# Hybrid attention encoder layer: the output projection in two groups of 1024 columns, with six of its sixteen row-pair products formed as seven products of block sums

## The chip, the cores and the metric

The kernel runs on one core of one Trainium2 chip. The metric is the device time of one execution in microseconds (us), the median of several runs. Before the change it is 1386.31 us (three runs, 1385.98 to 1386.63).

## The reference

The reference is one layer of an encoder on 256 tokens of 2048 numbers, in float32. Two attention branches and their gates come from one input projection; they are merged, projected, normed and added to the input, and a squared-ReLU MLP follows:

```
h = rms_norm(x, norm_mix_pre)
proj = h @ w_in                       # q, k, v of both branches, and the gates
oa = differential attention, on = neighbourhood attention
g_a, g_b = split(sigmoid(gates), 2)
mixed = g_a * (oa @ w_branch_a) + g_b * (on @ w_branch_b)
y = mixed @ w_out                     # 256 x 2048 by 2048 x 2048
x = x + rms_norm(y, norm_mix_post)
h = rms_norm(x, norm_mlp_pre)
u = square(relu(h @ w_up))
x = x + rms_norm(u @ w_down, norm_mlp_post)
```

The change touches `y = mixed @ w_out`, and what comes just before and behind it.

## The kernel before

The 256 tokens are two halves t0 and t1 of 128. Every float32 operand of a product is split in a high part of the matmul's own type and the remainder, the low part, and a product is three matmuls into one PSUM bank: high x high, high x low, low x high. ScalarE makes the high part (a copy that rounds), VectorE the low part (a subtraction). Weights come on SyncE's DMA queue in pieces of 1 MB, into pools of three buffers each for the raw piece, the high part and the low part (`wp`).

There are three ways of grouping a projection. `wgroup` (input projection, MLP up) has the weights stationary. `agroup` has the activations stationary and 512 columns of weights moving, in four pieces of four blocks of 128 rows each; both token halves accumulate in a bank of their own. `wide_group` (gates and branches) works on 1024 columns and on row pairs, that is 256 rows at a time, which makes a 2 x 2 block product of tokens (t0, t1) x rows by rows x columns. In the plain form (`eight`) a row pair is eight products. In the other (`seven`) it is seven products of sums of blocks, whose results five operations combine at the end (`combine`: a ScalarE copy and four VectorE operations over banks 0, 4, 5 and 6; the plain products go to banks 1, 2, 3 and 7, whose results are added piece by piece). `pair_weights` loads a pair's weights and, for `seven`, forms the sums of weight blocks on VectorE and splits them too; the two sums' parts are in a pool of five tiles (`mid`). `sums_of` forms the sums of activation blocks. The second to fourth gate groups use `seven` for three of their eight pairs (`MIXED`).

Around the output projection the order is as follows. The branch groups of the second column half (`bb1` last) end with the merged values in pages (a pool of 27 pages of 4 KB per partition). `mixed_T` transposes them on TensorE and splits them (`mh`, `ml`), the first half's earlier, the second half's 16 transposes at the start of y. The temporary pool `tmp` is opened again, `gpost` and `x2` (the post-norm gain and the residual input) are loaded on SP's queue. Then y runs as four `agroup`s of 512 columns (matmuls L230 to L232). Each group's `y_evac` squares the bank on ScalarE with a running sum, multiplies it by the gain on VectorE (L902), and in the last group calls `post_norm(t)`: a reduction, two small steps, and a power on GpSimd (L89).

In the last group t0 is finished before t1 begins. `residual_parts(t, c)` takes 512 columns: the residual on VectorE (L853), four transposes on TensorE (L860), and the split of each with the next norm's gain on ScalarE (L869) and VectorE (L870), into `hT2`, which the MLP's up projection reads. `between` puts the first two such blocks of t0 into t1's products, before the sixth and the seventh of the eight that are left; `tc.issue_after` ties the products behind them to that place. For t1 the first block (`residual_parts(1, 0)`) stands alone between y's last matmul and the first matmul of the up projection (L192); the other blocks are interleaved with the first up group.

A planner orders the instructions of each engine by a simulated timeline, with program order as priority, and gives pool tiles their places; each engine then runs its queue in that order.

Of the kernel before, what the change touches and what calls it, by code (L numbers as in the profile page):

```python
# [11 lines left out]
F32 = mybir.dt.float32  # L12
F32R = mybir.dt.float32r
AF = mybir.ActivationFunctionType
ALU = mybir.AluOpType
AX = mybir.AxisListType

P = 128
D = 2048
T = 256  # L20
KD = D // P
# [17 lines left out]
def encoder_layer(ctx: ExitStack, tc: tile.TileContext, a, out):  # L39
    nc = tc.nc  # L40
# [7 lines left out]
    temps = ctx.enter_context(ExitStack())  # L48
    tmp = temps.enter_context(tc.tile_pool(name="tmp", bufs=6))
    mm = ctx.enter_context(tc.tile_pool(name="mm", bufs=NMM, space=PSUM))  # L50
    ms = ctx.enter_context(tc.tile_pool(name="ms", bufs=8 - NMM, space=PSUM))

    def page(shape, dt, name):
        return pages.tile(shape, dt, tag="pg", name=name)
# [4 lines left out]
    def t2k(name, dt=F32):  # L59
        return tmp.tile([P, 2, T], dt, tag="t2k", name=name, bufs=7)  # L60
# [9 lines left out]
    def junk512(n):  # L70
        return tmp.tile([P, 2, T], F32, tag="t2k", name=n, bufs=7)
# [596 lines left out]
            nc.vector.tensor_sub(c12, self.ps[4], c12)  # L668
            nc.vector.tensor_sub(c22, self.ps[4], c21)

    def wide_group(name, kinds, view, stat7, stat8, mm_banks, z, piece, each=None):


        any7 = any(s for _, s in kinds)
        pr = Products(name, mm_banks, range(8) if any7 else (1, 2, 3, 7))
        for n, (i, seven) in enumerate(kinds):
            if each:
                each(n)
            w = pair_weights(view(i), f"{name}_{i}", seven)
            if seven:  # L680
                final = not any(s for _, s in kinds[n + 1 :])
                pr.seven(partial(stat7, i), w, final)
                if final:
                    pr.combine(z)
                continue
            end = n == len(kinds) - 1
            for which in range(4):
                pr.eight(partial(stat8, i), w, which, end)
                if end:
                    b, t, half = PLAIN[which]  # L690
                    piece(t, half, pr.ps[b], any7)

    def sums_of(p1, p2, name, hi=None, lo=None):

        a11, a21, a12, a22 = p1[:, :P], p1[:, P:], p2[:, :P], p2[:, P:]
        s = t2k(f"{name}s").rearrange("p a (b c) -> p (a b) c", b=2)
        nc.vector.tensor_sub(s[:, 0], a21, a22)
        nc.vector.tensor_sub(s[:, 1], a11, a21)
        nc.vector.tensor_sub(s[:, 2], s[:, 0], a11)
        nc.vector.tensor_add(s[:, 3], a12, s[:, 2])  # L700
        parts_ = page([P, 2, 4, P], F32R, name)
        nc.scalar.copy(parts_[:, 0], s)
        nc.vector.tensor_sub(parts_[:, 1], s, parts_[:, 0].bitcast(F32))
        return parts_
# [24 lines left out]
    ALL8 = [(i, 0) for i in range(8)]  # L729
    mT = []  # L730
    mixed = []

    def mixed_T(h, n):

        mh, ml = page([P, 4, T], F32R, f"mh{h}{n}"), page([P, 4, T], F32R, f"ml{h}{n}")
        for b in range(2):
            pt = bank(f"mT{h}{n}{b}")
            for j in range(2):
                for t in range(2):
                    c = (n * 4 + b * 2 + j) * P  # L740
                    nc.tensor.transpose(
                        pt[:, j * T + t * P : j * T + (t + 1) * P],
                        mixed[h][t].rearrange("p a b -> p (a b)")[:, c : c + P],
                        ident,
                    )
            at = slice(b * 2, b * 2 + 2)
            src = pt.rearrange("p (j q) -> p j q", j=2)
            nc.scalar.copy(mh[:, at], src)
            nc.vector.tensor_sub(ml[:, at], src, mh[:, at].bitcast(F32))
        mT.append((mh, ml))  # L750

    for h in range(2):
# [59 lines left out]
        mixed.append(gate[0])  # L812
    for n in range(2):
        mixed_T(1, n)
    stage.close()
    temps = ctx.enter_context(ExitStack())
    tmp = temps.enter_context(tc.tile_pool(name="tmp", bufs=6, reuse_waits="tile"))


    def mstat(k, t):  # L820
        mh, ml = mT[k // 4]
        return mh[:, k % 4, t * P : (t + 1) * P], ml[:, k % 4, t * P : (t + 1) * P]

    gpost = [page([P, 1024], F32, f"gpost{h}") for h in range(2)]
    for h in range(2):
# [4 lines left out]
    for t in range(2):  # L830
        for h in range(2):
            nc.sync.dma_start(
                x2[t * 2 + h], x[t * P : (t + 1) * P, h * 1024 : (h + 1) * 1024]
            )
    yw = [page([P, 1024], F32, f"yw{i}") for i in range(4)]
    ssy = [small(4, f"ssy{t}") for t in range(2)]

    ss2 = [small(4, f"ss2{t}") for t in range(2)]
# [10 lines left out]
    def residual_parts(t, c, after=None):  # L849
        cs = slice((c % 2) * 512, (c % 2 + 1) * 512)  # L850
        xt = x2[t * 2 + c // 2][:, cs]
        with tc.issue_after(after) if after else nullcontext():
            nc.vector.scalar_tensor_tensor(  # L853
                xt, yw[t * 2 + c // 2][:, cs], ry[:, t : t + 1], xt, op0=ALU.mult, op1=ALU.add
            )
        for h in range(2):
            pt = bank(f"h2T_t{t}{c}{h}")
            for i in range(2):
                kk = h * 2 + i
                last = nc.tensor.transpose(  # L860
                    pt[:, i * P : (i + 1) * P], xt[:, kk * P : (kk + 1) * P], ident
                )
            for i in range(2):
                k = c * 4 + h * 2 + i
                d = hT2[k // 2][:, k % 2]
                src = pt[:, i * P : (i + 1) * P]
                hi = d[:, t * P : (t + 1) * P]
                g = g_mlp[:, k : k + 1]
                act = nc.scalar.activation(hi, src, AF.Copy, scale=g)  # L869
                vec = nc.vector.scalar_tensor_tensor(  # L870
                    d[:, T + t * P : T + (t + 1) * P],
                    src,
                    g,
                    hi.bitcast(F32),
                    op0=ALU.mult,
                    op1=ALU.subtract,
                )
        return last.ins, act.ins, vec.ins

    def between(i):  # L880
        return residual_parts(0, i - 5)[0] if i in (5, 6) else None

    def mlp_squares(t):
        for c in range(4):
            cs = slice((c % 2) * 512, (c % 2 + 1) * 512)
            j = junk512("jx").rearrange("p a b -> p (a b)")
            nc.scalar.activation(
                j, x2[t * 2 + c // 2][:, cs], AF.Square, accum_out=ss2[t][:, c : c + 1]
            )
# [3 lines left out]
        nc.vector.tensor_reduce(s2, ss2[t], axis=AX.X, op=ALU.add)  # L893
        inv_rms(s2, D, f"r2{t}", r2[:, t : t + 1])

    for cg in range(4):

        def y_evac(t, ps, cg=cg):
            j = junk512("jy").rearrange("p a b -> p (a b)")
            nc.scalar.activation(j, ps, AF.Square, accum_out=ssy[t][:, cg : cg + 1])  # L900
            cs = slice((cg % 2) * 512, (cg % 2 + 1) * 512)
            nc.vector.tensor_mul(yw[t * 2 + cg // 2][:, cs], ps, gpost[cg // 2][:, cs])  # L902
            if cg == 3:
                post_norm(t)

        agroup(
            a["w_out"], cg * 512, mstat, KD, y_evac, f"y{cg}", *((2, between) if cg == 3 else ())
        )
    mlp_squares(0)
    tail = [residual_parts(1, 0)]  # L910
    after = {1: tail[0][1:]}
# [72 lines left out]
    for k in range(2, NK - LAST):  # L984
        w = dweight(k)
# [83 lines left out]
```

## Time and profile before

| | before |
|---|---|
| median of three runs | 1386.31 us |
| the profiled execution | 1386.53 us |
| its span, first to last instruction | 1384.7 us |
| mean granted TensorE clock | 0.996 |
| matmuls, weight loads | 6861 each |
| output projection, first to last matmul | 570.2 to 660.2 us |
| first matmul of the up projection | 665.0 us |

A row of the timeline gives the start in us from the span's start, the duration in us, the engine, the line of the kernel, the operation, what is written from what, and how many instructions were merged into the row; in brackets stands how long the engine had been idle and who released it. Matmul records overlap, since matmuls are pipelined: a 512-column one is shown as 0.39 us long, and they start about 0.23 us apart. A row of a table by stretch gives the stretch, its length, busy us with instruction counts for PE (matmuls), PEld (weight loads), DVE (VectorE), ACT (ScalarE) and POOL (GpSimd), the granted clock, the DMA share and GB/s.

### The profile page before, as it was taken

What the parts mean: (1) busy time and instruction counts of PE and PEld (TensorE: products, weight loads), DVE (VectorE), ACT (ScalarE), POOL (GpSimd) and SP (SyncE); (2) the same over time, 40 slices, a digit from 0 to 9 for tenths busy, and PEclk for the clock granted to TensorE, in tenths of its full rate; (3) what the DMA queues carried; (4) which work ended last, traced back from release to release, by engine and by line L of the source; (5) the groups of instructions that cost most, each with busy time, mean ns of one, the idle gap of its engine ahead of it and who ended that gap; (6) DMA issues with size and microseconds to landing.
All of it is one profiled execution on the core that took longest, in us unless ns stands there. A gap on an engine that the chain in (4) does not pass through costs nothing.

```text
span 1384.7 us, 16956 instructions
## 1 busy us (share of the span) xinstructions
PE 1363.7 (98%) x6861; PEld 1157.6 (84%) x6861; DVE 851.7 (62%) x1093; ACT 659.6 (48%) x923; POOL 7.9 (1%) x19
## 2 busy tenths in 40 slices
PE   7999999999999999999899999999999999999997
PEld 6888888888888888888788888888888888888886
DVE  6878866677857876654755554555566554444445
ACT  7455455544643544443754444444465443333332
POOL 0000000000000000000000000000000000000000
PEclk9999999999999999999999999999999999999999
DMA  8675745564655565766456565556555556555551
GB/s 292 204 230 165 205 153 182 178 180 156 206 187 184 208 223 172 248 225 195 127 178 212 161 205 184 196 189 192 182 183 208 186 191 235 183 196 199 186 200 71
DMA packets 105198, 265.11 MB, mean 191 GB/s; under 512 B 15008, under 2 KB 16288, under 8 KB 96928
## 3 DMA queue, kind: packets, MB, share of 16 engines
q1 hardware_dynamic: 104976, 264.03, 58.2%
q8 instruction: 53, 0.87, 0.3%
q14 instruction: 25, 0.20, 0.0%
q10 hardware_dynamic: 144, 0.01, 0.0%
HBM read 261.92 MB, written 3.92 MB: 192 GB/s over the span
## 4 chain that ended last, share of the span: by engine, by line
PE 98%; DVE 1%; DMA 0%; ACT 0%; SPq 0%; issue 0%; DVEq 0%; POOLq 0%; POOL 0%; ACTq 0%
PE u_p L192 17%; PE u_p L193 9%; PE acc L975 8%; PE acc L974 8%; PE acc L973 8%; PE qa_p L192 2%; PE ka_p L192 2%; PE qn_p L192 2%; PE kn_p L192 2%; PE ga L639 2%; PE y_p L232 2%; PE y_p L231 2%; PE ga L642 2%; PE ga L641 2%; PE y_p L230 2%; PE gb L642 2%
## 5 line engine op out<-in xcount | busy, mean ns | idle before, releaser
L192 PE MATMUL u_p<-h2T,u_h 128*128 128x512 f32 x1024 | 359.3, 397 | 1.0 <-DVE h2T L870 1.0
L193 PE MATMUL u_p<-h2T,u_l 128*128 128x256 f32 x1024 | 284.1, 280 | 0.0
L117 DVE TENSOR_TENSOR d_l<-d_w,d_h 128x1024 fp32r<-128x1024 f32 x128 | 151.1, 1222 | 164.1 <-ACT d_h L116 163.7
L117 DVE TENSOR_TENSOR u_l<-u_w,u_h 128x1024 fp32r<-128x1024 f32 x128 | 151.1, 1222 | 145.1 <-ACT u_h L116 143.8
L192 PEld LDWEIGHTS u_p<-h2T,u_h 128*128 128x128 f32 x1024 | 191.7, 188 | 45.7 <-DVE h2T L870 1.2
L116 ACT CAST d_h<-d_w 128x1024 fp32r<-128x1024 f32 x128 | 127.9, 1047 | 191.5 <-PE acc L975 187.9
L974 PE MATMUL acc<-d_l,uh 128*128 128x512 f32 x512 | 199.0, 389 | 0.0
L975 PE MATMUL acc<-d_h,ul 128*128 128x512 f32 x512 | 198.9, 389 | 0.0
L973 PE MATMUL acc<-d_h,uh 128*128 128x512 f32 x512 | 198.2, 389 | 0.0
L193 PEld LDWEIGHTS u_p<-h2T,u_l 128*128 128x128 f32 x1024 | 193.5, 189 | 1.3
L116 ACT CAST u_h<-u_w 128x1024 fp32r<-128x1024 f32 x128 | 128.0, 1048 | 123.1 <-PE u_p L192 62.3
L974 PEld LDWEIGHTS acc<-d_l,uh 128*128 128x128 f32 x512 | 96.1, 188 | 20.1
L973 PEld LDWEIGHTS acc<-d_h,uh 128*128 128x128 f32 x512 | 96.1, 188 | 19.9
L975 PEld LDWEIGHTS acc<-d_h,ul 128*128 128x128 f32 x512 | 96.1, 188 | 19.8
L117 DVE TENSOR_TENSOR y_l<-y_w,y_h 128x1024 fp32r<-128x1024 f32 x32 | 37.9, 1222 | 30.9 <-ACT y_h L116 30.9
L116 ACT CAST y_h<-y_w 128x1024 fp32r<-128x1024 f32 x32 | 32.0, 1047 | 40.9 <-PE y_p L232 32.6
L230 PE MATMUL y_p<-y_h,mh 128*128 128x512 f32 x128 | 50.1, 391 | 0.0
L231 PE MATMUL y_p<-y_l,mh 128*128 128x512 f32 x128 | 49.9, 390 | 0.0
L232 PE MATMUL y_p<-y_h,ml 128*128 128x512 f32 x128 | 49.8, 390 | 0.0
L192 PE MATMUL qa_p<-hT,qa_h 128*128 128x512 f32 x128 | 47.7, 419 | 1.2 <-DVE hT L275 1.2
L192 PE MATMUL qn_p<-hT,qn_h 128*128 128x512 f32 x128 | 45.9, 400 | 0.0
L192 PE MATMUL kn_p<-hT,kn_h 128*128 128x512 f32 x128 | 45.4, 398 | 0.0
(549 smaller groups left out, 2378.3 us busy)
## 6 DMA issues: line engine op xcount, KB each, us to landing
u_w<-in_w_up SPq DMA_DIRECT2D x64, 1024.0 KB, 5.4
d_w<-in_w_down SPq DMA_DIRECT2D x64, 1024.0 KB, 5.0
y_w<-in_w_out SPq DMA_DIRECT2D x16, 1024.0 KB, 5.3
ka_w<-in_w_in SPq DMA_DIRECT2D x8, 1024.0 KB, 6.7
va_w<-in_w_in SPq DMA_DIRECT2D x8, 1024.0 KB, 5.2
qn_w<-in_w_in SPq DMA_DIRECT2D x8, 1024.0 KB, 5.1
kn_w<-in_w_in SPq DMA_DIRECT2D x8, 1024.0 KB, 5.1
vn_w<-in_w_in SPq DMA_DIRECT2D x8, 1024.0 KB, 5.1
```

The source lines that it names most:

```text
L116: nc.scalar.copy(hi[part], raw[part])
L117: nc.vector.tensor_sub(lo[part], raw[part], hi[part].bitcast(F32))
L192: nc.tensor.matmul(ps[b], hi[:, k % 4, cs], mv, start=(k == 0), stop=False)
L193: nc.tensor.matmul(ps[b][:, :T], lo[:, k % 4, cs], mv[:, :T], start=False, stop=(k == nk - 1))
L230: nc.tensor.matmul(ps[t], sh, hi[:, k % 4], start=(k == 0), stop=False)
L231: nc.tensor.matmul(ps[t], sh, lo[:, k % 4], start=False, stop=False)
L232: nc.tensor.matmul(ps[t], sl, hi[:, k % 4], start=False, stop=(k == nk - 1))
L639: nc.tensor.matmul(self.ps[i], sh, wh[:, blk], start=i not in self.begun, stop=False)
L642: nc.tensor.matmul(self.ps[i], sl, wh[:, blk], start=False, stop=last)
L973: nc.tensor.matmul(acc[t][c], uh[:, k % 4, ts_], hi[:, 0, cs], start=(k == 0), stop=False)
L974: nc.tensor.matmul(acc[t][c], uh[:, k % 4, ts_], lo[:, 0, cs], start=False, stop=False)
L975: nc.tensor.matmul(acc[t][c], ul[:, k % 4, ts_], hi[:, 0, cs], start=False, stop=(k == NK - 1))
```

## The change

The output projection becomes two `wide_group`s of 1024 columns. Row pairs 1, 3 and 5 of each go as `seven`, the other five as `eight`. The activation sums for these pairs (`msum`) are formed in `mixed_T`, from a copy of the transposed values in a page. The results of the sevens are combined into `yw`; each piece of the plain products is then added to it by `y_piece`, squared from there and multiplied in place by the gain. The piece's scratch and the sums get pages, and `tmp` is opened again after y instead of before it.

In the second group the last two pairs are kept back and run together, one quarter (token half and column half) after the other, t0's two first; `between` is called within t1's quarters, and residual blocks of t0 stand before the sixth and seventh of t1's eight products, as before.

```diff
-    def wide_group(name, kinds, view, stat7, stat8, mm_banks, z, piece, each=None):
+    def wide_group(name, kinds, view, stat7, stat8, mm_banks, z, piece, each=None, between=None):
...
             end = n == len(kinds) - 1
+            if between and n == len(kinds) - 2:
+                ahead = (i, w)
+                continue
+            last = None
             for which in range(4):
-                pr.eight(partial(stat8, i), w, which, end)
+                if between and end:
+                    b, t, half = PLAIN[which]
+                    for m, (ii, ww) in enumerate((ahead, (i, w))):
+                        for k in range(2):
+                            if t:
+                                last = between((which - 2) * 4 + m * 2 + k) or last
+                            with tc.issue_after(last) if last else nullcontext():
+                                pr.add(b, stat8(ii, k, t), ww, k * 2 + half, m + k == 2)
+                else:
+                    pr.eight(partial(stat8, i), w, which, end)
                 if end:
                     b, t, half = PLAIN[which]
                     piece(t, half, pr.ps[b], any7)
...
-        s = t2k(f"{name}s").rearrange("p a (b c) -> p (a b) c", b=2)
+        s = page([P, 4, P], F32, f"{name}s")
...
+            i = h * 4 + n * 2 + b
+            if i in (1, 3, 5):
+                f = page([P, 512], F32, f"mf{i}")
+                nc.scalar.copy(f, pt)
+                msum[i] = sums_of(f[:, :T], f[:, T:], f"ms{i}")
...
-    for cg in range(4):
-
-        def y_evac(t, ps, cg=cg):
-            j = junk512("jy").rearrange("p a b -> p (a b)")
-            nc.scalar.activation(j, ps, AF.Square, accum_out=ssy[t][:, cg : cg + 1])
-            cs = slice((cg % 2) * 512, (cg % 2 + 1) * 512)
-            nc.vector.tensor_mul(yw[t * 2 + cg // 2][:, cs], ps, gpost[cg // 2][:, cs])
-            if cg == 3:
+    for g in range(2):
+
+        def y_piece(t, half, ps, summed, g=g):
+            z = yw[t * 2 + g][:, half]
+            nc.vector.tensor_add(z, z, ps)
+            j = page([P, 512], F32, f"jy{g}{t}{half}")
+            c = g * 2 + half
+            nc.scalar.activation(j, z, AF.Square, accum_out=ssy[t][:, c : c + 1])
+            nc.vector.tensor_mul(z, z, gpost[g][:, half * 512 : (half + 1) * 512])
+            if g and not half:
                 post_norm(t)
 
-        agroup(
-            a["w_out"], cg * 512, mstat, KD, y_evac, f"y{cg}", *((2, between) if cg == 3 else ())
-        )
+        wide_group(
+            f"y{g}",
+            [(0, 0), (1, 1), (2, 0), (3, 1), (4, 0), (5, 1), (6, 0), (7, 0)],
...
+            mstat7,
+            mstat8,
+            (1, 2, 3, 7),
+            [yw[g], yw[2 + g]],
+            y_piece,
+            between=between if g else None,
+        )
+    stage.close()
+    temps = ctx.enter_context(ExitStack())
+    tmp = temps.enter_context(tc.tile_pool(name="tmp", bufs=6, reuse_waits="tile"))
```

More of the change, by code (lines that the diff above doesn't have):

```diff
@@ L731, in encoder_layer @@
     mixed = []
+    msum = {}
     def mixed_T(h, n):
@@ L814, in encoder_layer, with mstat8, mstat7 @@
         mixed_T(1, n)
[L815 to L822, printed above, removed]
+    def mstat8(i, k, t):
+        mh, ml = mT[i // 2]
+        k = i % 2 * 2 + k
+        return mh[:, k, t * P : (t + 1) * P], ml[:, k, t * P : (t + 1) * P]
+    def mstat7(i, n):
+        if n < 3:
+            return mstat8(i, int(n > 0), n // 2)
+        return msum[i][:, 0, n - 3], msum[i][:, 1, n - 3]
     gpost = [page([P, 1024], F32, f"gpost{h}") for h in range(2)]
@@ L834, in encoder_layer @@
             )
-    yw = [page([P, 1024], F32, f"yw{i}") for i in range(4)]
+    yw = [page([P, 2, 512], F32, f"yw{i}") for i in range(4)]
     ssy = [small(4, f"ssy{t}") for t in range(2)]
@@ L853, in residual_parts @@
             nc.vector.scalar_tensor_tensor(
-                xt, yw[t * 2 + c // 2][:, cs], ry[:, t : t + 1], xt, op0=ALU.mult, op1=ALU.add
+                xt, yw[t * 2 + c // 2][:, c % 2], ry[:, t : t + 1], xt, op0=ALU.mult, op1=ALU.add
             )
@@ L894, in mlp_scale @@
         inv_rms(s2, D, f"r2{t}", r2[:, t : t + 1])
-    for cg in range(4):
-        def y_evac(t, ps, cg=cg):
-            j = junk512("jy").rearrange("p a b -> p (a b)")
-            nc.scalar.activation(j, ps, AF.Square, accum_out=ssy[t][:, cg : cg + 1])
-            cs = slice((cg % 2) * 512, (cg % 2 + 1) * 512)
-            nc.vector.tensor_mul(yw[t * 2 + cg // 2][:, cs], ps, gpost[cg // 2][:, cs])
-            if cg == 3:
-                post_norm(t)
-        agroup(
-            a["w_out"], cg * 512, mstat, KD, y_evac, f"y{cg}", *((2, between) if cg == 3 else ())
-        )
+    for g in range(2):
[7 more added lines that the diff above has]
+            if g and not half:
+                post_norm(t)
+        wide_group(
+            f"y{g}",
+            [(0, 0), (1, 1), (2, 0), (3, 1), (4, 0), (5, 1), (6, 0), (7, 0)],
+            lambda i, c=g * 1024: a["w_out"][i * T : (i + 1) * T, c : c + 1024].rearrange(
+                "(k p) c -> p k c", p=P
+            ),
+            mstat7,
[4 more added lines that the diff above has]
+            between=between if g else None,
+        )
+    stage.close()
+    temps = ctx.enter_context(ExitStack())
+    tmp = temps.enter_context(tc.tile_pool(name="tmp", bufs=6, reuse_waits="tile"))
     mlp_squares(0)
```

## The prediction

> **What bounds the kernel now.** I read the page's busy times and its chain of waits first, then a table by stretch of time around the output projection, and then the timeline of the projection's end.
>
> ```profile
> PE 1363.7 (98%) x6861; PEld 1157.6 (84%) x6861; DVE 851.7 (62%) x1093; ACT 659.6 (48%) x923; POOL 7.9 (1%) x19
> ...
> PE 98%; DVE 1%; DMA 0%; ACT 0%; SPq 0%; issue 0%; DVEq 0%; POOLq 0%; POOL 0%; ACTq 0%
> ```
>
> The first row is busy time by engine, the second the share of each in the chain that ended last: TensorE is the kernel. A change pays if it takes TensorE instructions away, and costs wherever it makes TensorE wait. The table by stretch shows the last two gate groups of the kernel before and then the whole output projection, y. Its columns are the stretch, its length, and busy us with instruction counts for PE, PEld, DVE, ACT, POOL.
>
> ```profile
> 441.60:483.00 41.40, 41.40 (x185) 34.28 (x184) 35.97 (x34) 21.81 (x17) 0.00 (x0) 1.00 0.60 206
> 483.00:524.50 41.50, 41.50 (x185) 34.38 (x184) 32.43 (x29) 20.54 (x17) 0.00 (x0) 1.00 0.62 203
> 570.00:660.20 90.20, 90.16 (x410) 74.36 (x408) 49.46 (x58) 38.87 (x56) 0.55 (x1) 1.00 0.66 222
> ```
>
> The gate groups already run as the change wants y to run: five row pairs in the plain form (8 products of 3 matmuls, 24) and three as seven products (21), so 5 x 24 + 3 x 21 = 183 matmuls; the count of 185 takes in instructions cut by the edges. TensorE was busy in all of the 41.40 us, so one 512-column matmul costs 41.40 / 183 = 0.2262 us, a plain pair 5.43 and a pair of seven 4.75. In y TensorE is busy without a gap for 90.16 us. What waits stands behind it:
>
> ```profile
> 653.81 0.60 ACT L900 ACTIVATE jy<-y_p 128x512 f32<-128x512 f32 x1 [3.44 <-PE y_p L232]
> 654.30 0.19 ACT L900 ACTIVATION_READ_ACCUMULATOR jy<-y_p 128x1 f32 x1
> 654.53 0.69 DVE L902 TENSOR_TENSOR yw<-y_p,gpost 128x512 f32<-128x512 f32 x1 [2.72 <-ACT jy L900]
> ...
> 656.13 1.42 DVE L853 SCALAR_TENSOR_TENSOR x<-yw,ry,x 128x512 f32<-128x512 f32 x2 [0.66 <-POOL ry L89]
> ...
> 657.01 0.60 PE L860 MATMUL h2T_t<-ident,x 128*128 128x128 f32 x4
> ...
> 660.20 0.60 ACT L900 ACTIVATE jy<-y_p 128x512 f32<-128x512 f32 x1
> 660.29 0.35 DVE L870 SCALAR_TENSOR_TENSOR h2T<-h2T_t,g_mlp,h2T 128x128 fp32r<-128x128 f32 x1 [0.17 <-ACT h2T L869]
> ...
> 660.92 0.69 DVE L902 TENSOR_TENSOR yw<-y_p,gpost 128x512 f32<-128x512 f32 x1 [0.28 <-ACT jy L900]
> ...
> 663.34 0.66 PE L860 MATMUL h2T_t<-ident,x 128*128 128x128 f32 x4 [3.17 <-DVE x L853]
> 664.99 0.80 PE L192 MATMUL u_p<-h2T,u_h 128*128 128x512 f32 x1 [0.99 <-DVE h2T L870]
> ```
>
> Each row is start, duration, engine and line. Token half t0 ends at 653.8; its norm and residual run beside t1's products and are ready at 656.13 + 0.74 = 656.87 (half of the 1.42 of two, with their overlap), 0.14 before its transposes start at 657.01. For t1 nothing covers the same steps: TensorE waits 3.17 and 0.99 us.
>
> **The change part by part.**
>
> *Matmuls removed.* Three of eight pairs in each of two groups go from 24 to 21: 6 x 3 = 18 matmuls x 0.2262 = **-4.07 us**, on the path because y has no gap. Weight loads go with their matmuls. The 16 transposes of the merge and the 8 of t0's residual stay; so do the bytes loaded.
>
> *Sums of weights and activations.* They go to VectorE and ScalarE and cost nothing where TensorE stays ahead. What one pair of seven costs, from the gate group:
>
> ```profile
> 452.28 1.76 DVE L617 TENSOR_TENSOR ga_3l<-ga_3r,ga_3h 128x1536 fp32r<-128x1536 f32 x1 [1.44 <-ACT ga_3h L613]
> 453.95 1.22 DVE L614 TENSOR_TENSOR ga_6t<-ga_6r 128x1024 f32<-128x1024 f32 x1
> 455.09 2.28 DVE L610 TENSOR_TENSOR ga_4l<-ga_4r,ga_4h 128x2048 fp32r<-128x2048 f32 x1
> 457.29 1.22 DVE L623 TENSOR_TENSOR ga_3el<-ga_3t,ga_3eh 128x1024 fp32r<-128x1024 f32 x1
> 458.42 0.68 DVE L615 TENSOR_TENSOR ga_6t<-ga_6t,ga_6r 128x512 f32<-128x512 f32 x1
> ...
> 459.81 0.39 PE L641 MATMUL ga<-ga_3el,hs 128*128 128x512 f32 x1
> ```
>
> VectorE needs 1.22 + 2 x 0.68 + 1.76 + 2 x 1.22 = 6.8 us for a pair of seven and 2.28 for a plain one. A group has 3 x 6.8 + 5 x 2.28 = 31.8, and its four combining and eight piece operations, about 0.69 each, bring 8.3: 40 by durations, which the gate group holds in 35.97 busy us (neighbours overlap) of 41.40. So VectorE goes from 49.46 / 90.2 to nearly nine tenths, and the cover is thin: ga_3el ends at 458.51 and is first used at 459.81, a lead of 1.30. Group y0 carries more than that gate group did:
>
> ```profile
> L749 DVE TENSOR_TENSOR ml<-mT,mh 128x512 fp32r<-128x512 f32 x4 | 2.5, 682 | 0.0
> ...
> L703 DVE TENSOR_TENSOR hs<-hs0s,hs 128x512 fp32r<-128x512 f32 x1 | 0.7, 685 | 0.0
> L697 DVE TENSOR_TENSOR hs3s<-hf 128x128 f32<-128x128 f32 x1 | 0.3, 293 | 0.0
> ```
>
> The last transposes of the merge are split in 2.5, and the sums of pair 5's activations take 4 x 0.29 + 0.69 = 1.8 (those of pairs 1 and 3 come a stage earlier). That is 4.3 more against a lead of 1.30, an idle 1.44 before ga_3l, and 1.22 + 2.28 of work for later pairs that was placed ahead of ga_3el. Bounds: 0 if later work gives way, 4.3 - 1.3 - 1.4 = 1.6 if it doesn't. I take **+0.2**, nearer to 0, since both gate groups lost nothing. Less than 0 is excluded: TensorE has no gap there to win back.
>
> *The moved pool and pages.* Temporaries reopen after y instead of before it; the square's scratch and the sums take pages. No row shows these; the nearest are the 35.97 and 32.43 rows, where the same two weight pools were open, and TensorE waited for nothing. I take 0; a page that comes late would hold x's or gpost's load on SP's queue, with y's weights behind it.
>
> *The end of t0.* A piece was: square from PSUM (0.60 + 0.19), then multiply (0.69). It becomes: add the partial result (nearest row L902, 0.69, the same size and engine), then square, then multiply in place, which must wait for the square. So t0's residual is 0.69 later against a slack of 0.14: TensorE, whose next product is ordered behind these transposes, waits 0.55. VectorE is fuller then than it was: pair 5's four combining operations (2.7), the first up weights (two pieces of 1.22) and the other half's add and multiply all fall in the 5 us before. If one weight piece is ahead of the add, the wait is 0.55 + 1.22 = 1.8. I take **+0.9**, bounds 0.5 and 1.8. What is late next is the t1 tail: the whole shift passes on to it.
>
> *The end of t1.* The add comes before the square on a bare chain: +0.69. In the kernel before, the square could start at 660.20 although VectorE was busy with t0's evacuations until 660.64; the add is on VectorE and must wait for these, which themselves start later while t1's first half brings an add and a multiply among them (2 x 0.69). Bounds 0.69 and 0.69 + 0.44 + 0.69 = 1.8; I take **+1.1**. ScalarE's squares of the residual go into the same idle time as before.
>
> *The clock.* The same table, in steps of 1 us, with the granted clock as the third number from the end:
>
> ```profile
> 664.00:665.00 1.00, 0.01 (x1) 0.01 (x1) 1.00 (x4) 0.47 (x3) 0.00 (x0) 0.97 0.00 0
> 665.00:666.00 1.00, 1.00 (x3) 0.91 (x4) 0.88 (x5) 1.00 (x3) 0.54 (x1) 0.50 0.00 0
> 666.00:667.00 1.00, 1.00 (x4) 0.81 (x4) 1.00 (x3) 1.00 (x2) 0.00 (x0) 0.50 0.00 0
> 667.00:668.00 1.00, 1.00 (x6) 0.90 (x5) 1.00 (x2) 0.48 (x1) 0.00 (x0) 0.50 0.00 0
> 668.00:669.00 1.00, 1.00 (x7) 0.96 (x6) 1.00 (x1) 0.62 (x2) 0.00 (x0) 0.82 0.07 16
> ```
>
> After the idle stretch TensorE runs at half clock for 0.03 x 2 + 3 + 0.18 x 2 = 3.4 us, nearly all of it with matmuls queued: 1.7 us lost. The loss can become less than this if part of the 3.4 us falls into a longer wait, so the bounds are -1.7 and 0. I take 0, the same loss again, since three runs within 0.65 us speak for one that comes back each time. [...]
>
> *The sum.* -4.07 + 0.2 + 0.9 + 1.1 = **-1.87 us** against the profiled execution, 1386.53. That execution is 0.22 above the median of the runs, 1386.31; from the median it is 1384.44. **Forecast: 1384.4 us**, 0.14% less. A measurement of this kernel can tell about 0.2%, 2.77 us, from no change, so this counts as no change.
>
> **The rivals.**
>
> *The slow stretch is hidden.* The wait for t1 grows from 3.2 us by about 1 and ends at another moment; if the clock has dropped well before TensorE resumes, some or all of the 1.7 us is spent waiting. 1384.4 - 1.7 = 1382.7. For it: the drop came only at about 664.97, at the very first up matmul, so that any shift can only shorten what is lost. Against it: the stretch may be tied to the idle time itself.
>
> *The tail costs only its two adds.* 0.5 for t0, 0.7 for t1, nothing at the start: -4.07 + 1.2 = -2.87, 1383.4. For it: the planner orders each engine's work and the add needs only one free slot. Against it: t0's evacuations filled VectorE until 0.44 after t1's last matmul already.
>
> *VectorE becomes the bound.* Place: the low parts of the summed weights (the second and third pair of seven in y0, the first and second in y1). If the 4.3 us of additional work aren't absorbed, each is late by the 1.6 above and VectorE never gets ahead again: 4 x 1.6 = 6.4 in place of 0.2 gives 1384.4 + 6.2 = 1390.6, slower. It decides from a lateness of about 1.2 at each of the four (4.64 in all: 1.87 won and 2.77 over). For it: the 1.30 lead. Against it: 36 of 41.4 us without one wait, and the first rows of that table start behind similar work.
>
> *All of it is given back.* t0 waits 1.8, t1 loses 1.8, the start 0.5: 1386.3, no change.
>
> **How the numbers follow.** The forecast case has 0.57, the hidden slow stretch 0.16, the adds alone 0.13, all given back 0.07, VectorE as bound 0.07. The forecast case's own range goes from its low bounds (-4.07 + 1.2, 1383.4) to its high ones (-4.07 + 1.6 + 1.8 + 1.8 = +1.1, 1387.4). The range for all is 1382.4 to 1387.4: it takes in the hidden stretch with 0.3 to spare, and leaves out the slower case and the corners. Faster by over 0.2% (below 1383.5): 0.16 + 0.13 and 0.04 of the forecast case, 0.33. Slower by over 0.2% (above 1389.1): the VectorE case, 0.07. Within it: 0.60.
>
> **What would show it.** Right: y's matmuls 366 instead of 384, the two groups at about 0.2262 each with no wait in y0; a wait of TensorE of 0.5 to 1.8 us before t0's first transposes; a wait of 4 to 5 us before t1's. Wrong: waits of y's matmuls for L623 or L617; no wait before t0's transposes; a shorter half-clock stretch behind the tail; loads of x or gpost that hold SP's queue so long that y's matmuls wait for a split.

## The result, and the profile after

The changed kernel takes 1395.59 us (median of four runs, 1394.78 to 1395.78) against 1386.14 for the kernel before (four runs, 1384.69 to 1386.63): ratio 1.0067, 95% interval 1.0055 to 1.0079. It is 9.45 us slower, where 1.87 less was forecast. Its profiled execution is the median run, 1395.59, with a span of 1393.8.

The page of the changed kernel, busy times and the chain of waits:

```profile
PE 1364.9 (98%) x6843; PEld 1157.1 (83%) x6843; DVE 888.7 (64%) x1138; ACT 672.5 (48%) x927; POOL 7.9 (1%) x19
...
PE 96%; DVE 2%; ACT 1%; issue 0%; DMA 0%; SPq 0%; POOL 0%; DVEq 0%; POOLq 0%; ACTq 0%
```

The 18 matmuls are gone (6861 to 6843), and yet TensorE is busy 1.2 us longer: some of its matmuls ran slower. Its share of the chain fell from 98 to 96%. What it waited for between 300 and 720 us (before, only the first and the last of these kinds were there, 3.2 and 1.0):

```profile
PE h2T_t L884 <- DVE x L877: 8.0, 2, 4.2
PE y L639 <- ACT y_4h L609: 2.1, 1, 2.1
PE y L641 <- DVE y_4l L610: 1.4, 1, 1.4
PE u_p L192 <- DVE h2T L894: 0.4, 1, 0.4
```

From y's first matmul to the first of the up projection it is 104.40 us (569.59 to 673.99) instead of 94.82 (570.17 to 664.99), 9.58 more: all of the loss lies here. It has two places. The first, in the first group (timeline; SPq is the DMA queue):

```profile
579.23 1.76 DVE L617 TENSOR_TENSOR y_3l<-y_3r,y_3h 128x1536 fp32r<-128x1536 f32 x1 [4.60 <-ACT y_3h L613]
...
587.32 2.29 DVE L610 TENSOR_TENSOR y_4l<-y_4r,y_4h 128x2048 fp32r<-128x2048 f32 x1 [0.88 <-ACT y_4h L609]
587.34 0.96 PE L639 MATMUL y<-y_4h,mh 128*128 128x512 f32 x3 [2.14 <-ACT y_4h L609]
589.53 1.22 DVE L614 TENSOR_TENSOR y_1t<-y_1r 128x1024 f32<-128x1024 f32 x1
589.64 0.38 SPq L606 DMA_DIRECT2D y_5r<-in_w_out  x1
589.67 0.79 PE L641 MATMUL y<-y_4l,mh 128*128 128x512 f32 x1 [1.36 <-DVE y_4l L610]
590.26 0.63 PE L642 MATMUL y<-y_4h,ml 128*128 128x512 f32 x1
590.69 0.63 PE L639 MATMUL y<-y_4h,mh 128*128 128x512 f32 x1
```

TensorE waits 2.14 and 1.36 us for pair 4, and then runs matmuls 0.43 apart instead of 0.23 until 595.4 (granted clock 0.50 from 590 to 595, 1.00 from 596 on). The row that tells why is y_1t: the first sums of pair 1's weights, whose piece was cast at 564, are formed only at 589.53, though VectorE stood idle for 4.60 us before 579.23. Without them TensorE had no other products left, and pairs 1 and 3 held two of the three raw buffers, so that pair 5's load left only at 589.64, when pair 4's piece was done with. The loads of gpost and x (574.47 to 577.74 on SPq) were not in the way: pair 4's load left ahead of them, at 574.05, and took 5.1 us to land.

The second place is the end of y:

```profile
657.49 0.69 DVE L924 TENSOR_TENSOR yw<-yw,y 128x512 f32<-128x512 f32 x1
658.62 0.69 DVE L924 TENSOR_TENSOR yw<-yw,y 128x512 f32<-128x512 f32 x1 [0.44 <-PE y L642]
659.23 0.69 DVE L928 TENSOR_TENSOR yw<-yw,gpost 128x512 f32<-128x512 f32 x1
659.83 0.68 DVE L924 TENSOR_TENSOR yw<-yw,y 128x512 f32<-128x512 f32 x1
660.43 0.68 DVE L928 TENSOR_TENSOR yw<-yw,gpost 128x512 f32<-128x512 f32 x1
661.30 0.69 DVE L928 TENSOR_TENSOR yw<-yw,gpost 128x512 f32<-128x512 f32 x1
662.72 1.41 DVE L877 SCALAR_TENSOR_TENSOR x<-yw,ry,x 128x512 f32<-128x512 f32 x2 [0.66 <-POOL ry L89]
663.52 1.02 PE L884 MATMUL h2T_t<-ident,x 128*128 128x128 f32 x4 [3.81 <-DVE x L877]
...
672.45 1.11 PE L884 MATMUL h2T_t<-ident,x 128*128 128x128 f32 x4 [4.16 <-DVE x L877]
673.99 0.80 PE L192 MATMUL u_p<-h2T,u_h 128*128 128x512 f32 x1 [0.42 <-DVE h2T L894]
```

t0's last product is added at 658.62 and t0's transposes run at 663.52: TensorE waits 3.81 us. Between them VectorE's queue holds the addition and the multiply of t1's first piece (659.83, 661.30), and TensorE had only five matmuls of t1 behind t0's last product, not the 15 that the kernel before has: in the order that the planner wrote, ten others stand ahead of it. Then t1's wait, 4.16. With both waits the granted clock falls from 1.00 to 0.50; with the second (table by stretch in steps of 1 us, granted clock third from the end):

```profile
670.00:671.00 1.00, 0.00 (x0) 0.00 (x0) 0.93 (x4) 0.00 (x1) 0.00 (x0) 0.75 0.00 0
...
676.00:677.00 1.00, 1.00 (x6) 0.90 (x5) 1.00 (x2) 0.64 (x1) 0.00 (x0) 0.50 0.00 0
677.00:678.00 1.00, 1.00 (x7) 0.95 (x6) 1.00 (x1) 0.62 (x2) 0.00 (x0) 0.84 0.00 0
```

This stretch goes from about 670.5 to 677.3, 6.8 us, twice the 3.4 of the kernel before; there is one of 6.8 in the first group (588.6 to 595.4) and one of 3.4 behind t0's wait (663.7 to 667.1), where the kernel before has none (1.00 from 570.0 to 660.2).

### The profile page after: what moved, and what is told of

It is laid out like the page before. It is cut to its first block, busy times and chain, and to the rows that moved or that the text cites. A ratio compares the mean times of both kernels' runs of the same rounds, so it can differ in the third digit from the quotient of the medians.

```text
span 1393.8 us, 16981 instructions
## 1 busy us (share of the span) xinstructions
PE 1364.9 (98%) x6843; PEld 1157.1 (83%) x6843; DVE 888.7 (64%) x1138; ACT 672.5 (48%) x927; POOL 7.9 (1%) x19
## 4 chain that ended last, share of the span: by engine, by line
PE 96%; DVE 2%; ACT 1%; issue 0%; DMA 0%; SPq 0%; POOL 0%; DVEq 0%; POOLq 0%; ACTq 0%
PE u_p L192 17%; PE u_p L193 9%; PE acc L1014 8%; PE acc L1013 8%; PE acc L1012 8%; PE qa_p L192 2%; PE ka_p L192 2%; PE qn_p L192 2%; PE kn_p L192 2%; PE ga L641 2%; PE ga L642 2%; PE ga L639 2%; PE gb L642 2%; PE gb L641 2%; PE gb L639 2%; PE y L641 2%
## 5 line engine op out<-in xcount | busy, mean ns | idle before, releaser
L192 PE MATMUL ka_p<-hT,ka_h 128*128 128x512 f32 x128 | 45.0, 398 | 0.0
L997 ACT ACTIVATE u<-up_s 128x256 f32<-128x256 f32 x64 | 25.1, 418 | 25.3 <-DVE up_s L996 25.2
L255 ACT COPY up_r<-u_p 128x256 f32<-128x256 f32 x64 | 23.6, 369 | 26.1 <-PE u_p L193 26.0
L193 PE MATMUL qn_p<-hT,qn_l 128*128 128x256 f32 x128 | 35.9, 281 | 0.0
L193 PE MATMUL kn_p<-hT,kn_l 128*128 128x256 f32 x128 | 35.7, 280 | 0.0
```

The lines of the kernel that those rows point to most:

```text
L192: nc.tensor.matmul(ps[b], hi[:, k % 4, cs], mv, start=(k == 0), stop=False)
L193: nc.tensor.matmul(ps[b][:, :T], lo[:, k % 4, cs], mv[:, :T], start=False, stop=(k == nk - 1))
L255: nc.scalar.copy(r, ps[:, T:])
L997: nc.scalar.activation(u[:, b], s, AF.Square)
```

## The experiments

My theory was that what makes the first place is the order in which the page pool hands out its pages: in the order of the program, so that a tile called for later in the program gets none before those called for earlier. Pair 1's sums, called for with the first group's weights, would then stand behind the pages of the merge's last transposes and of gpost and x. For the second place I had three suspects: the queue orders around t0's norm, the combination just ahead of it, and VectorE's load. The rival throughout was the load: VectorE has too much to do, whatever the order.

All runs are timed against the kernel before on the same chip; the difference is in us of medians. The runs were made on several chips, so rows are best compared by this column.

| run | what it is | median | differs by | ratio, 95% |
|---|---|---|---|---|
| after | the change | 1395.59 | +9.45 | 1.0055 to 1.0079 |
| e1 | first group's weights asked for earlier | 1389.75 | +3.33 | 1.0016 to 1.0037 |
| e2 | square's scratch in the bank | 1399.56 | +13.14 | 1.0084 to 1.0112 |
| e3 | e1 and e2 | 1392.58 | +6.16 | 1.0033 to 1.0061 |
| e4 | t1's products behind t0's | 1394.86 | +8.44 | 1.0050 to 1.0075 |
| e5 | e1, t0's norm ahead of t1's piece | 1388.27 | +2.07 | 1.0005 to 1.0023 |
| e6 | e5 and e4's order | 1387.66 | +1.46 | 1.0001 to 1.0019 |
| e7 | e6, multiply not in place, u's parts later | 1389.01 | +2.81 | 1.0009 to 1.0027 |
| e8 | e1, second group plain | 1385.54 | -0.66 | 0.9984 to 1.0002 |
| e9 | e8, MLP squares behind t1's | 1384.03 | -2.36 | 0.9976 to 0.9994 |
| e10 | the change, second group plain | 1391.73 | +5.34 | 1.0025 to 1.0050 |
| e11 | e6, sevens earlier, squares as e9 | 1391.18 | +4.79 | 1.0025 to 1.0050 |
| e12 | e11, residual first | 1391.51 | +5.12 | 1.0024 to 1.0051 |
| e13 | e8, MLP squares' scratch in pages | 1384.60 | -1.43 | 0.9980 to 0.9998 |
| e14 | e6, squares as e9 | 1387.60 | +1.57 | 1.0000 to 1.0018 |
| e15 | e14 with five sevens | 1386.16 | +0.13 | 0.9992 to 1.0009 |

**e1, the order of the pages.**

```diff
+    made = {i: pair_weights(a["w_out"][i * T : (i + 1) * T, :1024]..., f"y0_{i}", bool(i % 2)) for i in range(4)}
     for n in range(2):
         mixed_T(1, n)
```

> The weights of the first group's first four row pairs are asked for, in program order, ahead of the merge's last transposes; nothing else is changed. Theory (pages): the pool hands its pages out in program order, so the sums of pair 1's weights stood behind the parts of the merge's last transposes and the loads of gpost and x. If so, the two waits in the first group (2.14 and 1.36 us) and the half-clock stretch behind them (2.8 us lost) go: 1395.6 - 6.3 = 1389.3 us, and perhaps 1 to 2 less as VectorE carries less arrears into the second group. Rival (load): VectorE simply has more work in the first group than TensorE's time; then the hole only moves to another operand and the time stays at 1394 to 1396 us.

Measured 1389.75, 5.84 us less than the change. The order of calls is all that differs, and the sums come 33 us earlier (VectorE's timeline), on an engine that has the same work:

```profile
556.01 1.22 DVE L614 TENSOR_TENSOR y_1t<-y_1r 128x1024 f32<-128x1024 f32 x1 [5.14 <-DMA y_1r<-in_w_out]
```

The waits of TensorE in e1; of the first group's 3.5 us nothing is left, 0.4 us at 628.7 us, in the second group, is new, and t0's 3.81 and t1's 3.93 stay (7.7 in two):

```profile
PE h2T_t L890 <- DVE x L883: 7.7, 2, 3.9
PE u_p L192 <- DVE h2T L900: 0.4, 1, 0.4
PE y L641 <- DVE y_4l L610: 0.4, 1, 0.4
```

The load is ruled out for the first place. e10, below, shows the same loss alone. That it is the pool that holds the sums is not shown apart: program order is also the planner's priority, and e1 moves both. For the pool speaks that VectorE idled with the piece at hand, which priority alone does not explain, and that in e13, below, a change of pool alone moves other tiles.

**e2 and e3, the scratch pages of the second group.**

```diff
-            j = page([P, 512], F32, f"jy{g}{t}{half}")
-            nc.scalar.activation(j, z, AF.Square, accum_out=...)
+            nc.scalar.activation(ps, z, AF.Square, accum_out=...)
```

> The square's scratch output goes back into the PSUM bank that was just read instead of a page; nothing else is changed. Theory (pages): in the second group the sums of pair 1's weights stood behind the first group's four scratch pages. Without them these sums come some 10 us earlier, pair 7's low part no longer comes late, and the 3.81 us wait before t0's first transposes falls to 0.6 to 1.8 us: 1392.4 to 1393.6 us, with the hole in the first group unchanged. Rival (load): VectorE is full from 587 us on whatever the order, and the time stays within 0.5 us of 1395.6.

> Both edits: the first four row pairs' weights are asked for ahead of the merge's last transposes, and the square's scratch goes into the bank. Theory (pages): both gains add, 1395.6 - 6.3 - 2 to 3 = 1386 to 1387.5 us, with no wait inside the first group and 0.5 to 1.8 us before t0's first transposes. Rival (load): 1393 us or more, with the waits at other operands.

Measured 1399.56 and 1392.58: both misses, each slower than the kernel without the edit (by 3.97 and 2.83). The sums did come earlier, as the theory has it (618.21 instead of 626.25 in the second group), so the pages hold sums there too. But a new wait arose:

```profile
PE y L639 <- ACT y L926: 2.3, 1, 2.3
```

The second group's first products wait 2.3 us for a bank, and a half-clock stretch of 3.4 us follows (e2, granted clock 0.50 from 626.2 to 629.6). Two things make this wait. The earlier sums stand ahead of the first group's last additions on VectorE, three of which begin only at 624.55 (in the change one at 619.38 and two at 621.64). And the bank is now free only when ScalarE has squared the piece (from 625.27), not when VectorE has added it. What each of the two cost is not shown. t0's wait stayed at 3.9 although the sums came 8 us earlier, so the scratch pages are not its cause. The runs say nothing on what the pages alone would bring there.

**e4, e5, e6: what makes t0's transposes late.** e4 puts t1's products of the last two pairs behind t0's last one. e5 leaves TensorE alone and, on e1, puts t1's first addition behind t0's norm on VectorE. e6 does both.

```diff
+                if between and end and which == 2:
+                    last = done                      # e4, e6: t0's last product
...
+            with tc.issue_after(scaled["ry0"]) if g and t and half else nullcontext():   # e5, e6
                 nc.vector.tensor_add(z, z, ps)
```

> The change's kernel with one order more: t1's products of the last two row pairs stand behind t0's last product, so that 15 matmuls (3.4 us) of t1 lie between t0's last product and t0's transposes, where the changed kernel has 5 (1.1 us). Theory (order): the wait before t0's transposes comes from the cover that was lost and falls from 3.81 by 1.6 to 2.3 us: 1393.3 to 1394.0 us. Rival (VectorE's queue): t0's pieces are held by the combination of the sevens, which VectorE ends only at 657.5; the order of TensorE's products changes only the 0.44 us that VectorE waited for TensorE: 1395.2 us.

> As e1, and on VectorE the addition of t1's first piece (and with it its square and multiply) stands behind the last VectorE step of t0's norm; TensorE's order is not touched. Theory (queue order): in e1 that addition and multiply, 0.6 us each, lie between t0's own steps, so the wait before t0's transposes falls from 3.81 by 1.2 to 2.6 or 2.1 us: 1388.0 to 1388.5 us with the half-clock stretch behind the wait, 1386 if that goes too. Rival (late products): t0's chain is set by when t0's last product ends, and the time stays at 1389.5 to 1390.

> As e5, and t1's products of the last two row pairs stand behind t0's last product (the order of e4), so that 15 matmuls instead of 5 plus 3 lie between it and t0's transposes. Theory: with VectorE no longer in arrears both orders are needed together; the wait before t0's transposes falls to about 1 us and the half-clock stretch behind it (some 2.3 us lost) goes: 1389.75 - 2.6 - 2.3 = 1384.9 us. Rival (VectorE's load): the combination of the sevens and the first up weights' parts hold t0's pieces whatever the order; a gain of 1.7 us or less over e1, 1388 us or more.

e4 measured 1394.86, near the rival's 1395.2, with t0's wait at 3.20 instead of 3.81: with VectorE in arrears, TensorE's order is worth about 0.7. e5 measured 1388.27, 1.5 less than e1, and t0's wait went from 3.81 to 2.79, as the steps taken out of the chain make it. e6 measured 1387.66: the wait is 1.98, not about 1, and the half-clock stretch behind it did not go (0.50 from 656.2 to 659.6). The waits in e5 and e6:

```profile
656.26 0.73 PE L892 MATMUL h2T_t<-ident,x 128*128 128x128 f32 x4 [2.79 <-DVE x L885]
...
655.77 0.73 PE L894 MATMUL h2T_t<-ident,x 128*128 128x128 f32 x4 [1.98 <-DVE x L887]
```

What seems left in the way is the combination (e6, VectorE; L668 to L671 combine, L935 adds, L939 multiplies); e15, below, bears it out:

```profile
648.78 0.68 DVE L668 TENSOR_TENSOR yw<-yw,y 128x512 f32<-128x512 f32 x1
649.49 0.69 DVE L669 TENSOR_TENSOR yw<-yw,y 128x512 f32<-128x512 f32 x1
650.10 0.68 DVE L935 TENSOR_TENSOR yw<-yw,y 128x512 f32<-128x512 f32 x1
650.69 0.68 DVE L670 TENSOR_TENSOR yw<-y,yw 128x512 f32<-128x512 f32 x1
651.29 0.68 DVE L671 TENSOR_TENSOR yw<-y,yw 128x512 f32<-128x512 f32 x1
651.89 0.68 DVE L935 TENSOR_TENSOR yw<-yw,y 128x512 f32<-128x512 f32 x1
652.49 0.68 DVE L939 TENSOR_TENSOR yw<-yw,gpost 128x512 f32<-128x512 f32 x1
```

Six operations 0.6 us apart stand back to back ahead of t0's first multiply, and none of them waits for TensorE. They begin as the first up weights' parts are done, at 648.86. Pair 5's last product of sums ends at 648.1 (647.74 + 0.39 on TensorE), so they could begin some 0.6 us earlier, but no more.

**e7, two more steps off the chain.**

```diff
+    after = {0: combined[-1:], 1: tail[0][1:]}     # u's first parts behind the combination
...
+                m = gained[t] = page([P, 512], F32, f"yg{t}")   # multiply into another page
```

> As e6, and two more: the parts of the first up weights stand behind the combination of the sevens, and the gain multiply of each half's last piece writes another page, so that it need not wait for the square. Theory: t0's pieces can be added as soon as TensorE has them (1.06 us earlier), and the multiply leaves t1's bare chain (0.6 us): 1384.9 - 0.6 = 1384.3 us, with less than 0.5 us before t0's transposes and 3.3 instead of 3.9 before t1's. Rival: the steps beside them end last, and the time is e6's within 0.3.

A miss: 1389.01, 1.35 more than e6. The combination could not begin before 648.34, as VectorE then waited 2.09 us for TensorE; the up weights' parts that had filled this time (646.50 to 648.86 in e6) now stood at 651.73, between the combination and t0's last addition, and t0's wait grew from 1.98 to 3.18. t1's wait fell by 0.3, from 4.01 to 3.70. The two edits were made together, so that only these waits tell them apart.

**e8, e9, e13: the second group plain, and ScalarE's queue.** e8 is e1 with eight plain pairs in the second group.

```diff
-            [(0, 0), (1, 1), (2, 0), (3, 1), (4, 0), (5, 1), (6, 0), (7, 0)],
+            ALL8 if g else [(0, 0), (1, 1), (2, 0), (3, 1), (4, 0), (5, 1), (6, 0), (7, 0)],
```

> As e1, but the second group has no sevens: eight plain row pairs, its pieces squared and multiplied straight from the banks as in the kernel before; 9 matmuls removed in all, 2.04 us. Theory: what is left of the loss in e1 comes from the sevens of the second group (their combination, the additions of the pieces, VectorE's load just ahead of t0's norm); without them t0's transposes don't wait, t1's wait is the old 3.2 us, and the time is 1386.4 - 2.04 + 0.4 (the small wait left in the first group) = 1384.8 us. Rival (the form): the wide form with its two pairs run together delays t0's norm by itself; a wait of over 1 us before t0's transposes and 1386.5 us or more.

Measured 1385.54; t0 no longer waits at all. With 9 matmuls (2.04 us) more than e1 it is 4.21 us faster (3.99 by the table's differences), so the second group's sevens cost e1 about 6 us. But t1's wait was 4.42:

```profile
PE h2T_t L890 <- DVE x L883: 4.4, 1, 4.4
PE u_p L192 <- DVE h2T L900: 0.5, 1, 0.5
```

ScalarE's timeline in e8 shows the MLP squares of t0 (jx, L917; four of them, from 653.75 to 656.7) ahead of t0's second block of parts (L899) and of the square of t1's last piece (L935):

```profile
653.75 0.63 ACT L917 ACTIVATE jx<-x 128x512 f32<-128x512 f32 x1
...
656.73 1.13 ACT L899 ACTIVATE h2T<-h2T_t,g_mlp 128x128 fp32r<-128x128 f32 x4
657.73 0.61 ACT L935 ACTIVATE jy<-y 128x512 f32<-128x512 f32 x1
```

In the kernel before they run behind it, at 660.79. e9 orders them there; e13 only takes their scratch from the pages, in which the last piece's scratch stands ahead of them in the program.

```diff
+    with tc.issue_after(sq[0]):                      # e9: the square of t1's last piece
         mlp_squares(0)
```

```diff
-            j = junk512("jx").rearrange("p a b -> p (a b)")
+            j = page([P, 512], F32, f"jx{t}{c}")     # e13, no order written
```

> As e8 (second group plain), and ScalarE's four MLP squares of token half t0 stand behind the square of t1's last piece, where the kernel before has them by itself. In e8 they ran at 653.8 to 656.7, ahead of t0's second block of parts and of t1's last square, and t1's wait was 4.42 us instead of 3.17. Theory (ScalarE's queue): the wait falls to about 3.3 us and the time to 1384.3 us. Rival (VectorE's queue): the wait comes from VectorE's own steps for t0; no change, 1385.5 us.

> As e8, and the scratch of the MLP squares is taken from the pages instead of the pool of temporaries, with no order written; nothing else. Theory (pool order): a tile is handed out only behind those of the same pool that come before it in the program, so that behind the last piece's scratch page the squares stand behind t1's last square by themselves, as in e9: 1384.0 us and a wait for t1 of about 3.2 us. Rival: the place of the squares has nothing to do with their pool; 1385.5 us as e8.

Measured 1384.03 and 1384.60. Both have the waits of the kernel before (shown for e9):

```profile
PE h2T_t L890 <- DVE x L883: 3.2, 1, 3.2
PE u_p L192 <- DVE r_m L86: 1.0, 1, 1.0
```

So the change's other pool edit, opening the temporaries behind y, let the squares go ahead; the tile's pool alone puts them back. e9 and e13 are the versions that beat both kernels: 0.9976 to 0.9994 and 0.9980 to 0.9998 of the kernel before. Which of the two is better is not shown.

**e10, the first place alone.** The changed kernel with a plain second group, and its sums late.

> The changed kernel with a plain second group and nothing else: e8 without the earlier request of the first group's weights. Theory: the first group's hole and the half-clock stretch behind it are a cost of their own, 3.5 + 2.8 us, less the 0.0 to 0.4 that e8 still waits there: 1385.5 + 6.2 = 1391.7 us, with no wait before t0's transposes. Rival: most of the loss needs the second group's load too; 1389 us or less.

Measured 1391.73, as expected to 0.03, with the waits of 2.1 and 1.4 for y_4 and no wait for t0. Between e10 and e8 lie 6.2 us by their medians (6.0 by their differences from the kernel before), between the change and e1 5.8: the first place adds to the second and doesn't need it.

**e11, e12: the sevens earlier.**

```diff
+            [(1, 1), (0, 0), (3, 1), (2, 0), (5, 1), (4, 0), (6, 0), (7, 0)] if g else [...]
...
+            with tc.issue_after(xin[0]) ...          # e12 only: behind t0's residual
```

> As e6, all six pairs as sevens, with two more edits in the second group: its row pairs go in the order 1, 0, 3, 2, 5, 4, 6, 7, so that the combination stands three plain pairs ahead of the end instead of two, and t0's MLP squares stand behind t1's last square (e9). Theory: t0's wait falls from 1.98 to about 1 us without the half-clock stretch behind it (1.7 us), t1's from 4.01 by 0.4: 1387.7 - 1.0 - 1.7 - 0.4 = 1384.6 us. Rival (load): VectorE cannot deliver the sums of weights that much earlier and TensorE waits for them at the start of the second group; 1387 us or more.

> As e11, and the addition of t1's first piece stands behind t0's residual on VectorE, not only behind the last small step of t0's norm: in e11 the residual can be held by that addition, which waits for a product that ends 2.7 us after t0's last. Theory: t0's wait falls by another 0.4 us, 1384.2 us. Rival: the addition wasn't in the way; e11's time within 0.3 us.

Measured 1391.18 and 1391.51, the rival's side. The waits in e11:

```profile
PE h2T_t L894 <- DVE x L887: 4.8, 2, 4.0
PE y L641 <- ACT y_2h L611: 2.3, 1, 2.3
PE y L643 <- DVE y_0l L612: 0.9, 1, 0.9
...
PE y L641 <- ACT y_3h L615: 0.4, 1, 0.4
```

t0's wait did fall, to 0.8 (4.8 in two, one of them 4.0). But the sums of the second group's first pair now fall into the time in which VectorE combines, adds and multiplies the first group's results (610 to 623 us); TensorE waits 3.6 us there, and a half-clock stretch follows (mean granted clock 0.66 from 625 to 630). That is the rival's place. But load is not shown to be the whole cause:

```profile
605.85 1.75 DVE L619 TENSOR_TENSOR y_1l<-y_1r,y_1h 128x1536 fp32r<-128x1536 f32 x1
610.36 0.69 DVE L668 TENSOR_TENSOR yw<-yw,y 128x512 f32<-128x512 f32 x1 [2.77 <-PE y L644]
...
618.08 1.22 DVE L616 TENSOR_TENSOR y_1t<-y_1r 128x1024 f32<-128x1024 f32 x1
```

From 610.36 on VectorE is busy nearly without a gap, but just before it had idled for 2.77 us, with pair 1's weights at hand (split at 605.85), and their first sums came at 618.08. What held them is open; as in the first place, other pages stand ahead of theirs in the program, those of the first group's squares among them. In e12 t0's wait fell by another 0.24 us, to 0.53, but t1's grew by 0.43, to 4.44, and the time stayed: the addition had been a little in the way, and moving it gains nothing.

**e14, e15: what is left of e6.**

> As e6 (all six pairs as sevens, t0's products and norm first), with t0's MLP squares behind t1's last square as in e9. Theory: the squares cost here what they cost in e8, 1.5 us: 1387.7 - 1.5 = 1386.2 us, the rest over e9 being the combination ahead of t0's norm. Rival: with six sevens the end is set by VectorE, not by ScalarE's queue; 1387.2 us or more.

> As e14 with pair 5 of the second group plain: five sevens, 15 matmuls removed (3.39 us), and the combination stands behind pair 3, four plain pairs ahead of the end. Theory (combination): t0's wait falls to 0.8 us, without a half-clock stretch behind it, and t1 pays for its addition alone: 1386.4 - 3.4 + 0.4 + 0.8 + 0.7 = 1384.9 us. Rival (second group's load as a whole): waits of 2 us or more stay before t0's transposes, 1386 us or more.

e14 measured 1387.60, e6's time: with six sevens the squares' place is worth nothing, the rival's side. e15 measured 1386.16. t0's wait is the 0.77 expected, without a half-clock stretch behind it (granted clock 1.00 from 655 to 660):

```profile
654.18 0.66 PE L894 MATMUL h2T_t<-ident,x 128*128 128x128 f32 x4 [0.77 <-DVE x L887]
```

e15 also takes pair 5's sums off VectorE, but e11 keeps them, has the combination one plain pair earlier than e14, and has the same wait; together they point to the place of the combination as what held t0. e15's time is 1.3 above the theory. In its profile, of a run of 1385.49, t1's wait (4.01, then 0.70) is followed by 6.8 us of half clock (661.6 to 668.4) instead of the 3.4 of e9, some 1.7 us more by estimate; that this is the difference is not shown. Against e9, two more sevens take 6 matmuls (1.36 us) away and cost 3.5 to 3.9.

## Why the prediction was wrong, point by point

*Matmuls removed, -4.07.* Right: 18 fewer, 0.2262 us each at full clock.

*Sums of weights and activations, +0.2.* Wrong at its place. The bound of 1.6 took VectorE's load to decide when a sum is formed. What decided was their place in the order of calls: they were formed 33 us later than in e1. With that mended (e1), no wait is left in the first group, and 0.4 in the second. The load itself was put too low: a piece of the gate group takes one operation on VectorE, not two, so the 35.97 us hold four piece operations and not eight, and a group of y asks 4 x 0.69 = 2.8 us more. In the change VectorE was busy in 42.35 of the 45.40 us from 613.20 to 658.60.

*The moved pool and pages, "I take 0".* This is the step that failed. The 0 was taken from the gate groups, where the same weight pools were open, but where no last transposes, gpost or x stand ahead of the sums in the program. I looked for a page that comes late under gpost's and x's loads, not for weight sums that come late behind them. It cost 5.8 to 6.2 us (e1, e10): 3.5 of waiting and by estimate some 2.8 of half clock, about half of the 11.3 us between the forecast of -1.87 and the +9.45 measured. The other half of the same step, the temporaries opened behind y, cost 0.8 to 1.7 in the plain version (e8 against e13 and e9) and nothing that can be measured with six sevens (e14).

*The end of t0, +0.9.* The mechanism was right in part, VectorE fuller ahead of t0's norm; its size was not, and TensorE's cover, 15 matmuls behind t0's last product, was taken as unchanged and became 5. The wait was 3.81, of which 1.0 was t1's own piece in t0's chain (e5) and 0.8 the cover lost on TensorE (e6); most of the remaining 1.98 is the combination (0.77 with it further ahead, e15 and e11). I had counted the combination's 2.7 us as work in the 5 us before, but not that it cannot begin before the last product of sums ends.

*The end of t1, +1.1.* About right in size: from y's last matmul to u's first 6.08 instead of 5.22, +0.86. That ScalarE's squares go into the same idle time as before was wrong: in the change they run from 663.56 on, ahead of t1's last square at 669.28.

*The clock, 0, with bounds -1.7 and 0.* Wrong in sign, and a second term that failed. Half-clock stretches stand behind the added waits in the first group and for t0 (6.8 and 3.4 us), and the old stretch doubled (3.4 to 6.8). TensorE was busy 1.2 us longer with 4.07 us less work, so that slower matmuls cost some 5.3 us in all by estimate, 2.8 of them in the first group. I argued from the steadiness of three runs that the loss comes back the same; it does in e9 and e13, where the waits for t1 are those of the kernel before (3.2 and 1.0) and the stretch is again 3.4 us long.

*The rivals.* "VectorE becomes the bound" (0.07) is the nearest, 1390.6, but for its place: in the first group VectorE had idle time, and in the second the order of its queue and the combination made most of t0's wait. The first sign of being wrong was to be y's matmuls waiting for L623 or L617; they waited for L609 and L610, the parts of pair 4's plain weights, as without the sums no other products were left. No rival had a tile pool as its cause.

What stays open: how e14's and e15's loss over e9 splits between the half clock and the additions at t1's end, which one profile of each does not tell apart from the spread of the runs (1.2 to 3.2 us within these kernels); and what holds the second group's sums until the first group's results are dealt with (e2, e11).

## What to carry to other kernels

Where a pool hands out tiles in program order, as the runs here suggest, moving a temporary into it, or opening it elsewhere, moves every later tile of that pool in time: before counting an engine's load, list for each pool what stands ahead of the tile that the busiest engine needs. A saving of products that is paid for on another engine should be taken in the stage with slack and not in the one that ends on a bare chain: of the six pairs here, the three in the first group gave their 2 us (e9), and those in the second cost about three times what they gave (e1 against e8, e14 against e9).

## What the runs showed of the hardware that was not expected

The stretches at a granted clock of 0.50 behind t1's wait are of three lengths, worked out from the rows in steps of 1 us: 3.4 us in the kernel before, e9 and e13, 6.8 in the change, e8 and e15, 10.2 in e14 (661.2 to 671.4). Two waits for t0 of nearly equal length differ. In e6 TensorE idles for 1.98 us, and from 656.2 to 659.6 the clock is at 0.50:

```profile
655.00:656.00 1.00, 0.23 (x2) 0.23 (x3) 1.00 (x2) 0.84 (x3) 0.00 (x0) 1.00 0.05 20
656.00:657.00 1.00, 1.00 (x6) 0.90 (x5) 1.00 (x3) 1.00 (x5) 0.00 (x0) 0.62 0.00 0
```

In e14 it idles for 2.01 us before the same transposes, and the clock stays at 1.00 until 661.2:

```profile
655.00:656.00 1.00, 0.00 (x0) 0.00 (x0) 0.93 (x3) 0.72 (x2) 0.21 (x1) 1.00 0.01 2
656.00:657.00 1.00, 0.95 (x6) 0.88 (x7) 1.00 (x2) 0.48 (x2) 0.00 (x0) 1.00 0.00 0
```

What tells the two apart is not shown. The stretches behind t1's wait differ in the waits that fall into them. In the kernel before and in e9, where they are 3.4 us long, TensorE waits for less than 0.1 us in them. In e8 and e15, where they are 6.8 us long, the wait of 0.54 and of 0.70 us before the first up matmul lies in them, and in the change, of 6.8 us too, the last 2.0 us of the wait of 4.16 and the 0.42 behind it. In e14, where it is 10.2 us long, it begins 2.5 us before the transposes (663.73) and also holds a wait of 0.53 us. What sets the length is not shown; each of these is a single profile. A wait with such a stretch behind it is dearer than its length: by estimate 1.7 us for every 3.4 us that TensorE works through at 0.50, with matmuls 0.43 us apart instead of 0.23 (the change, from 590.26 to 594.95).
